# A YOCO decoder step on one core: the last three output tiles by halves of the tokens

## The chip, the cores and the metric

The kernel runs on one core of one Trainium2 chip. The metric is the device time of one execution in microseconds (us), as a median of several runs; beside it stands one execution that was recorded by the hardware profiler, and all rows of the profile come from that one. Its "span" is the time from the first to the last instruction of the core.

## What is computed

One inference step of a two-layer decoder over 512 prompt tokens and 8 sample tokens (520 columns in all), width 1024, hidden width 2816. Each layer adds half a SwiGLU, a mixer, and half a SwiGLU again; the kernel works through four SwiGLU blocks, and the fourth is followed by the last RMSNorm, whose rows are the outputs `y_prompt` and `y_sample`:

```python
def _rmsnorm(x, g):
    xf = x.astype(jnp.float32)
    y = xf * lax.rsqrt(jnp.mean(xf * xf, axis=-1, keepdims=True) + EPS)
    return (y * g.astype(jnp.float32)).astype(x.dtype)
...
        x = x + 0.5 * _swiglu(_rmsnorm(x, norm_g[l, 2]), ffn_w_gate[l, 1], ffn_w_up[l, 1], ffn_w_down[l, 1])
    y = _rmsnorm(x, final_norm_g)
```

Everything is float32. The sum of squares over the width of 1024 can be known only when all of a token's outputs are there.

## The kernel before

The activations lie transposed: `x[m]` (m = 0 to 7) holds 128 of the 1024 features in the partitions and the 520 tokens in the columns, and `H` = 260 is half of the tokens. A product in full precision is three matmuls, since activations and weights are each split into a high and a low part (`th`/`tl`, `hh`/`hl`, `wh`/`wl`); `mm` (L406) issues the three terms for one slice of weights, each for the two halves of the tokens, into the two banks of a pair. There are four such pairs of PSUM banks, handed out by `duo` (L224); a pair is free again when all that reads it is done. Transposes and sums for 1/rms take pairs from the same four.

**Weights.** `Weights` (L95) loads chunks of weights into three buffers `raw` and splits them, piece by piece, into six buffers `wh` and six `wl` (ScalarE at L191, VectorE at L192). `get` hands out the next piece, `prefetch` splits up to five pieces ahead. A piece's buffer is free for the sixth next one when its matmuls are done.

**One SwiGLU block** is `ffn` (L556). It goes through the hidden width in three parts of 8, 8 and 6 tiles; in each part it computes the hidden tiles (`plain_tile`, `strassen_tile`, with the matmuls at L435), then adds the part's share to all eight output tiles (the matmuls at L410). The first two output tiles are interleaved, so that the last hidden tile is needed late (L573 to L584); the others go one by one through `mm_tile` (L418). For each tile, L589 scales the result by 1/rms of the block's input (`u`, from PSUM) and L590 adds it to `x[m]`. In the last part, `after(m)` is called for each tile. With six hidden tiles an output tile of the last part takes 6 x 3 x 2 = 36 matmuls of 260 columns and two pieces of weights.

**The end of the kernel.** In the fourth block `after` is `final_after` (L1265). For tile k it takes the squares on ScalarE (`square`, L363), adds them to `acc` on VectorE (L367), and scales `x[k]` by the norm's weight into `xg` (ScalarE, L1268). Then it calls `turn` (L1245) for the tile that waits, and lets tile k wait. So tile 0 is turned when tile 1 is through, and so on. `turn` transposes one `xg` on TensorE, four times 128 tokens (L1250) and a last 120 (L1251), and copies the five results from PSUM to the output rows `yt`, by turns on VectorE (L1261) and ScalarE (L1259). After the last turn, `rstd_tok` (L372) sums the squares over the partitions with five small matmuls (L378) and computes 1/rms of all tokens in twelve tiny VectorE operations (L382 to L389). At last, ten half rows are scaled in place (VectorE L1283, ScalarE L1281) and stored, one DMA each, half of them from SyncE's queue and half from ScalarE's (L1287, L1289).

**What sets the order.** The kernel is written in an order of its own, but each engine's queue is filled by the framework's scheduler, which simulates the program and may put an instruction ahead of others that it takes to be ready later. `later` (L248) pins an instruction behind all that was written before it for its engine. Once the queues are fixed, each engine works through its own in order; an instruction whose data aren't there holds up all behind it.

## Time and profile before

| what | value |
|---|---|
| time, median of 3 runs | 1728.08 us (1722.71 to 1731.19) |
| the profiled execution, its own time | 1729.8 us |
| its span | 1728.0 us |
| mean granted clock of TensorE | 0.98 |
| TensorE busy (PE) | 97% of the span |
| VectorE (DVE), ScalarE (ACT) busy | 73%, 52% |
| DMA | 227.06 MB, mean 131 GB/s |

How to read the rows below: in the timeline, a row is start, duration, engine, line, operation, output and inputs, and in brackets how long the engine stood idle before it and what ended that. In the chain, a row is start, time on the path in us, engine, output and line (with the count of instructions merged into it). In the stretches, there follow on each stretch its length, the busy time of PE, PEld (weight loads), DVE, ACT and POOL with their instructions, the granted clock of TensorE, the DMA engines' busy share and GB/s. In the groups, a row is line, engine, operation, tiles, shapes and count, then busy us and the mean of one in ns, then the idle time before. ACTq and SPq are the queues from which ScalarE and SyncE issue DMAs.

### The profile page before, as it was taken

How to read it: one execution, taken by the hardware profiler on the slowest of the kernel's cores; microseconds unless marked ns; L12 is line 12 of the kernel's file. 1: busy time of each engine (PE TensorE's matmuls, PEld its weight loads, DVE VectorE, ACT ScalarE, POOL GpSimd, SP SyncE). 2: the span in 40 equal slices, each digit the busy share in tenths (PEclk: the TensorE clock that was granted, in tenths of full speed). 3: DMA queues.
4: the chain of work that ended last, by engine and by line, in shares of the span. 5: the costliest groups of instructions: out<-in, count | busy, mean ns of one | idle time of the engine just before them, and what ended most of it. 6: DMA issues, size and time to landing. Idle time of an engine off the chain costs nothing.

```text
span 1728.0 us, 34367 instructions
## 1 busy us (share of the span) xinstructions
PE 1669.6 (97%) x13701; PEld 1654.0 (96%) x13701; DVE 1269.1 (73%) x2454; ACT 904.7 (52%) x1810; POOL 146.1 (8%) x178
## 2 busy tenths in 40 slices
PE   7999999999899999999999999998889999999996
PEld 7999999999899999999999999998779899999996
DVE  6966866877875875887866866878756785785765
ACT  6643634656552643655543634647855653462553
POOL 0101101001001101001101101100000110110100
PEclk9999999999999999999999999999979999999998
DMA  8646746663445845546646746642112465666531
GB/s 204 159 129 141 171 135 144 180 183 75 102 141 132 182 134 135 141 128 145 155 127 141 174 135 141 155 140 50 25 35 73 111 163 144 146 150 159 135 86 51
DMA packets 315872, 227.06 MB, mean 131 GB/s; under 512 B 9265, under 2 KB 290969, under 8 KB 315671
## 3 DMA queue, kind: packets, MB, share of 16 engines
q1 hardware_dynamic: 285872, 174.82, 35.5%
q0 software_dynamic: 23200, 41.82, 14.7%
q10 hardware_dynamic: 6638, 8.23, 1.5%
q8 instruction: 107, 1.75, 0.4%
q14 instruction: 55, 0.44, 0.1%
HBM read 180.89 MB, written 5.04 MB: 108 GB/s over the span
## 4 chain that ended last, share of the span: by engine, by line
PE 67%; DVE 4%; ACT 3%; issue 0%; ACTq 0%; DVEq 0%
PE ps L435 35%; PE ps L410 30%; ACT sm L1034 1%; DVE sm L1019 1%; PE ps L1075 1%; DVE wl L192 1%; PE ps L1159 0%; PE ps L1052 0%; DVE xl L243 0%; ACT xh L242 0%; PE ps L1127 0%; DVE rp L856 0%; ACT wh L191 0%; PE ps L1250 0%; ACT oT L1087 0%
## 5 line engine op out<-in xcount | busy, mean ns | idle before, releaser
L191 ACT ACTIVATE wh<-raw 128x512 fp32r<-128x512 f32 (+1 forms) x742 | 449.6, 621 | 542.8 <-PE ps L410 326.3
L192 DVE TENSOR_TENSOR wl<-raw,wh 128x512 fp32r<-128x512 f32 (+1 forms) x742 | 491.0, 677 | 206.9 <-ACT wh L191 202.2
L435 PE MATMUL ps<-th,wh 128*128 128x260 f32 x1264 | 358.4, 284 | 5.4 <-ACT th L242 3.7
L435 PE MATMUL ps<-tl,wh 128*128 128x260 f32 x1264 | 358.7, 284 | 0.4 <-DVE tl L243 0.4
L435 PE MATMUL ps<-th,wl 128*128 128x260 f32 x1264 | 356.5, 283 | 0.6 <-DVE wl L192 0.5
L410 PE MATMUL ps<-hh,wh 128*128 128x260 f32 x1376 | 282.1, 286 | 4.0 <-DVE mx L1019 3.0
L410 PE MATMUL ps<-hl,wh 128*128 128x260 f32 x1376 | 280.9, 284 | 0.0
L410 PE MATMUL ps<-hh,wl 128*128 128x260 f32 x1376 | 279.4, 283 | 0.0
L435 PEld LDWEIGHTS ps<-th,wh 128*128 128x128 f32 x1264 | 238.9, 189 | 6.7 <-ACT th L242 4.1
L435 PEld LDWEIGHTS ps<-tl,wh 128*128 128x128 f32 x1264 | 239.4, 189 | 1.3 <-DVE tl L243 1.3
L435 PEld LDWEIGHTS ps<-th,wl 128*128 128x128 f32 x1264 | 238.6, 189 | 1.0 <-DVE wl L192 1.0
L410 PEld LDWEIGHTS ps<-hh,wh 128*128 128x128 f32 x1376 | 213.4, 190 | 5.4 <-DVE mx L1019 3.6
L410 PEld LDWEIGHTS ps<-hl,wh 128*128 128x128 f32 x1376 | 215.0, 190 | 0.0
L410 PEld LDWEIGHTS ps<-hh,wl 128*128 128x128 f32 x1376 | 214.0, 189 | 0.0
L435 PE MATMUL ps<-xh,wh 128*128 128x260 f32 x708 | 198.9, 283 | 0.6 <-ACT wh L191 0.6
L435 PE MATMUL ps<-xl,wh 128*128 128x260 f32 x708 | 198.6, 283 | 0.0
L435 PE MATMUL ps<-xh,wl 128*128 128x260 f32 x708 | 194.7, 282 | 1.0 <-DVE wl L192 1.0
L156 POOL DMA_DIRECT2D raw<-raw x79 | 68.4, 866 | 1389.1 <-DVE wl L192 504.7
L589 DVE TENSOR_TENSOR u<-ps,R 128x520 f32<-128x520 f32 x96 | 67.0, 698 | 107.5 <-PE ps L410 107.5
L435 PEld LDWEIGHTS ps<-xh,wh 128*128 128x128 f32 x708 | 133.6, 189 | 1.0 <-ACT wh L191 0.8
L435 PEld LDWEIGHTS ps<-xl,wh 128*128 128x128 f32 x708 | 133.5, 189 | 0.0
L435 PEld LDWEIGHTS ps<-xh,wl 128*128 128x128 f32 x708 | 131.4, 189 | 1.4 <-DVE wl L192 1.4
(237 smaller groups left out, 2845.7 us busy)
## 6 DMA issues: line engine op xcount, KB each, us to landing
raw<-in_ffn_w_gate_dram SPq DMA_DIRECT2D x87, 512.0 KB, 4.1
raw<-in_ffn_w_up_dram SPq DMA_DIRECT2D x87, 512.0 KB, 5.4
raw<-in_ffn_w_down_dram SPq DMA_DIRECT2D x32, 1024.0 KB, 4.9
raw<-raw POOLq DMA_DIRECT2D x79, 256.0 KB, 3.3
S<-in_ffn_w_up_dram SPq DMA_DIRECT2D x79, 256.0 KB, 5.5
S<-raw POOLq DMA_DIRECT2D x79, 256.0 KB, 4.6
raw<-in_ffn_w_down_dram SPq DMA_DIRECT2D x16, 768.0 KB, 6.2
raw<-in_w_q_dram SPq DMA_DIRECT2D x8, 512.0 KB, 6.7
```

The source lines that it names most:

```text
L156: G.dma_start(blk(raw, 2, 1), blk(raw, 1, 1), accum_op=ALU.add)
L191: nc.scalar.activation(dh, src, AF.Copy)
L192: nc.vector.tensor_tensor(dl, src, dh.bitcast(F32), op=ALU.subtract)
L410: T.matmul(banks[:, hf, :H], a[:, kk, :], hcols(b, hf), start=(first and i == 0), stop=(last and i == 2),)
L435: T.matmul(bank[:, :H], a[:, kk, :], b, start=(not more and kk == 0 and i == 0), stop=(kk == 3 and i == 2), skip_group_check=more,)
L589: V.tensor_tensor(halves(u), banks[m][:, :, :H], halves(R), op=ALU.mult)
L1019: V.tensor_tensor_reduce(out=sm[:, e * 256 : (e + 1) * 256], in0=self.pe[e][:, bi * 256 : (bi + 1) * 256], in1=cst[:, mk : mk + 256], op0= ...
L1034: S.activation(part(i), part(i), AF.Exp, bias=nm[:, i : i + 1], accum_out=den[:, i : i + 1])
L1075: T.matmul(po[:, bi * 256 : (bi + 1) * 256], a, p_[:, kc_], start=(n == 0), stop=(n == 3 * len(kts) - 1),)
```

## The change

`ffn` takes a further argument, `by_halves`. In the last part of the fourth block the tiles 0 to 4 go as before. Tiles 5 to 7 (`NH` = 3) are computed for the first 260 columns, each with its own addition to `x` and its call of `by_halves(m, 0)`, and then for the other 260 with `by_halves(m, 1)`; their six pieces of weights and three bank pairs are kept from the first pass to the second. The pairs of all tiles from 2 on are now taken one at a time rather than two at a time.

Two tiles wait before one is turned (three in the list before the first is taken), so tile 0 is turned when tile 2 is through. `turn` can do a range of token blocks; its copies from one bank are a single operation, on VectorE for even tiles and ScalarE for odd ones, and the block of 120 is copied by the other engine. `final_half` does squares, sum and `xg` of one half; in the first halves it turns the tiles 3 and 4, and the first two token blocks of 5 and 6; behind tile 5's second half follow those of tile 7 and 1/rms of those 256 tokens (`rstd_tok(0, 2)`); behind tile 6's second half those rows are scaled and stored, and the remaining blocks of tiles 5, 6 and 7 are turned one behind the other. At the end `rstd_tok(2)` and the stores of blocks 4, 2 and 3 follow.

```diff
@@ -369,24 +370,22 @@
     pss_ = [None]
     nsb = [4]
 
-    def rstd_tok():
+    def rstd_tok(t0=0, t1=5):
 
         pss_[0] = duo()
         pss = pss_[0][:, 0, :]
-        for t in range(5):
+        for t in range(t0, t1):
             lo = t * P if t < 4 else 400
             T.matmul(pss[:, t : t + 1], acc[:, lo : lo + P], ones[:, 0:1], start=True, stop=True)
-        v = cp.tile([P, 5], F32, tag="nv", name="nv")
-        y = cp.tile([P, 5], F32, tag="ny", name="ny")
-        t1 = cp.tile([P, 5], F32, tag="nt", name="nt")
-        later(V.tensor_scalar(v, pss[:, :5], 1.0 / D, EPS, op0=ALU.mult, op1=ALU.add))
+        v, y, t_ = (cp.tile([P, 5], F32, tag=n, name=n)[:, t0:t1] for n in ("nv", "ny", "nt"))
+        later(V.tensor_scalar(v, pss[:, t0:t1], 1.0 / D, EPS, op0=ALU.mult, op1=ALU.add))
         V.tensor_scalar(y.bitcast(I32), v.bitcast(I32), 1, None, op0=ALU.arith_shift_right)
         V.tensor_scalar(y.bitcast(I32), y.bitcast(I32), -1.0, float(0x5F3759DF), op0=ALU.mult, op1=ALU.add)
         for it in range(3):
-            V.tensor_tensor(t1, y, y, op=ALU.mult)
-            V.scalar_tensor_tensor(t1, t1, -0.5, v, op0=ALU.mult, op1=ALU.mult)
-            o = r_tok[:, :5] if it == 2 else y
-            V.scalar_tensor_tensor(o, t1, 1.5, y, op0=ALU.add, op1=ALU.mult)
+            V.tensor_tensor(t_, y, y, op=ALU.mult)
+            V.scalar_tensor_tensor(t_, t_, -0.5, v, op0=ALU.mult, op1=ALU.mult)
+            o = r_tok[:, t0:t1] if it == 2 else y
+            V.scalar_tensor_tensor(o, t_, 1.5, y, op0=ALU.add, op1=ALU.mult)
 
     def rstd_all():
 
@@ -553,7 +552,7 @@
             split(tt[k + 4], t34)
             yield
 
-    def ffn(fi, tmp, mov, hooks, tt, tags, after, before_last=None):
+    def ffn(fi, tmp, mov, hooks, tt, tags, after, before_last=None, by_halves=None):
 
         j = 0
         for pi, n in enumerate(PARTS):
@@ -568,30 +567,47 @@
                     strassen_tile(tmp, mov, tt, hs)
                 j += 1
             nk = (n + 1) // 2
-            for m0 in range(0, KT, 2):
-                banks = {m: duo() for m in (m0, m0 + 1)}
-                if m0 == 0:
-                    late = []
-                    for m in (0, 1):
-                        for k0, k1 in ((0, nk), (nk, n)):
-                            w = W.get()
-                            for k in range(k0, min(k1, n - 1)):
-                                mm(w, k - k0, hs[k], banks[m], k == 0, False)
-                            finish()
-                        late.append((w, m))
-                    for w, m in late:
-                        mm(w, n - 1 - nk, hs[n - 1], banks[m], False, True)
-                    W.prefetch()
-                for m in (m0, m0 + 1):
-                    if m0:
-                        mm_tile(hs, banks[m])
-                    u = tmp.tile([P, TOK], F32, tag="sb", name="u", bufs=nsb[0])
-                    V.tensor_tensor(halves(u), banks[m][:, :, :H], halves(R), op=ALU.mult)
-                    V.scalar_tensor_tensor(x[m], u, -0.5, x[m], op0=ALU.mult, op1=ALU.add)
-                    if last:
-                        if before_last is not None:
-                            next(before_last, None)
-                        after(m)
+            rest = NH if last and by_halves is not None else 0
+
+            def add(m, bank, hfs):
+                c = slice(hfs[0] * H, (hfs[-1] + 1) * H)
+                u = tmp.tile([P, TOK], F32, tag="sb", name="u", bufs=nsb[0])[:, c]
+                parts = lambda z: z.rearrange("p (h c) -> p h c", c=H)
+                V.tensor_tensor(parts(u), bank[:, hfs[0] : hfs[-1] + 1, :H], parts(R[:, c]), op=ALU.mult)
+                V.scalar_tensor_tensor(x[m][:, c], u, -0.5, x[m][:, c], op0=ALU.mult, op1=ALU.add)
+
+            banks = {m: duo() for m in (0, 1)}
+            late = []
+            for m in (0, 1):
+                for k0, k1 in ((0, nk), (nk, n)):
+                    w = W.get()
+                    for k in range(k0, min(k1, n - 1)):
+                        mm(w, k - k0, hs[k], banks[m], k == 0, False)
+                    finish()
+                late.append((w, m))
+            for w, m in late:
+                mm(w, n - 1 - nk, hs[n - 1], banks[m], False, True)
+            W.prefetch()
+            for m in range(KT - rest):
+                if m > 1:
+                    banks[m] = duo()
+                    mm_tile(hs, banks[m])
+                add(m, banks[m], (0, 1))
+                if last:
+                    if before_last is not None:
+                        next(before_last, None)
+                    after(m)
+
+            ws = {}
+            for hf in range(2 if rest else 0):
+                for m in range(KT - rest, KT):
+                    if not hf:
+                        banks[m] = duo()
+                        ws[m] = W.get(), W.get()
+                    for k in range(n):
+                        mm(ws[m][k // nk], k % nk, hs[k], banks[m], k == 0, k == n - 1, (hf,))
+                    add(m, banks[m], (hf,))
+                    by_halves(m, hf)
 
     def ff_pool():
         return tc.tile_pool(name="ff", bufs=2)
@@ -1240,53 +1256,82 @@
     kvs.close()
 
     with ff_pool() as tmp:
-        tt, yt = {}, {}
-
-        def turn(k, xg):
+        tt = {}
+
+        yt = [tmp.tile([P, 4, 512], F32, name="yt", bufs=1)]
+        ys = []
+        xgs, waiting = {}, []
+
+        def turn(k, t0=0, t1=5):
 
             pd = duo()
             pa, pb = pd[:, 0, :], pd[:, 1, :]
-            for t in range(4):
-                T.transpose(pa[:, t * P : (t + 1) * P], xg[:, t * P : (t + 1) * P], ident)
-            T.transpose(pb[:120, :P], xg[:, 400:520], ident)
-            for t in range(5):
-                n = P if t < 4 else 120
-                if k % 4 == 0:
-                    yt[t, k // 4] = big.tile([P, 512], F32, tag=XX[k // 4], name="yt")
-                dst = yt[t, k // 4][:n, (k % 4) * P : (k % 4 + 1) * P]
-                src = pa[:, t * P : (t + 1) * P] if t < 4 else pb[:120, :P]
-                if t % 2:
-                    S.copy(dst, src)
-                else:
-                    V.tensor_copy(dst, src)
-
-        waiting = []
+            for t in range(t0, min(t1, 4)):
+                T.transpose(pa[:, t * P : (t + 1) * P], xgs[k][:, t * P : (t + 1) * P], ident)
+            if t1 > 4:
+                T.transpose(pb[:120, :P], xgs[k][:, 400:520], ident)
+            if k == 4 and len(yt) < 2:
+                yt.append(rawp.tile([P, 4, 512], F32, tag="raw", name="yt1"))
+            if t1 > 4 and k % 4 == 0:
+                ys.append(big.tile([P, 512], F32, tag=XX[k // 4], name="ys"))
+            cols = slice((k % 4) * P, (k % 4 + 1) * P)
+            dst = yt[k // 4][:, t0 : min(t1, 4), cols]
+            src = pa.rearrange("p (t c) -> p t c", t=4)[:, t0 : min(t1, 4), :]
+            one, other = (S.copy, V.tensor_copy) if k % 2 else (V.tensor_copy, S.copy)
+            one(dst, src)
+            if t1 > 4:
+                other(ys[k // 4][:120, cols], pb[:120, :P])
+
+        def scaled(k, c):
+            if k not in xgs:
+                xgs[k] = tmp.tile([P, TOK], F32, tag=("t", "sa")[k % 2], name="xg")
+            S.activation(xgs[k][:, c], x[k][:, c], AF.Copy, scale=gcol(N_FIN, k))
 
         def final_after(k):
             square(k, tmp, "g")
-            xg = tmp.tile([P, TOK], F32, tag="t", name="xg")
-            S.activation(xg, x[k], AF.Copy, scale=gcol(N_FIN, k))
-            if waiting:
-                turn(*waiting.pop())
-            waiting.append((k, xg))
-
-        ffn(3, tmp, mov6, start_hooks(tmp, 5, tt, 1), tt, HH, final_after)
-        turn(*waiting.pop())
-        rstd_tok()
-        for t in range(5):
-            n = P if t < 4 else 120
-            for a in range(2):
-                y = yt[t, a][:n, :]
-                if a:
-                    S.activation(y, y, AF.Copy, scale=r_tok[:n, t : t + 1])
-                else:
-                    V.tensor_scalar(y, y, r_tok[:n, t : t + 1], None, op0=ALU.mult)
-                cols = slice(a * 512, (a + 1) * 512)
-                eng = nc.sync if a else nc.scalar
-                if t < 4:
-                    eng.dma_start(y_prompt[0, t * P : (t + 1) * P, cols], y)
-                else:
-                    eng.dma_start(y_sample[:, 0, cols], yt[t, a][112:120, :])
+            scaled(k, slice(0, TOK))
+            waiting.append(k)
+            if len(waiting) > 2:
+                turn(waiting.pop(0))
+
+        def store(tiles):
+            for t in tiles:
+                n = P if t < 4 else 120
+                for a in range(2):
+                    y = yt[a][:, t, :] if t < 4 else ys[a][:120, :]
+                    if a:
+                        S.activation(y, y, AF.Copy, scale=r_tok[:n, t : t + 1])
+                    else:
+                        V.tensor_scalar(y, y, r_tok[:n, t : t + 1], None, op0=ALU.mult)
+                    cols = slice(a * 512, (a + 1) * 512)
+                    eng = nc.sync if a else nc.scalar
+                    if t < 4:
+                        eng.dma_start(y_prompt[0, t * P : (t + 1) * P, cols], y)
+                    else:
+                        eng.dma_start(y_sample[:, 0, cols], ys[a][112:120, :])
+
+        def final_half(k, hf):
+            c = slice(hf * H, (hf + 1) * H)
+            sq = tmp.tile([P, TOK], F32, tag="g", name="sq")
+            S.activation(sq[:, c], x[k][:, c], AF.Square)
+            V.tensor_tensor(acc[:, c], acc[:, c], sq[:, c], op=ALU.add)
+            scaled(k, c)
+            if not hf and waiting:
+                turn(waiting.pop(0))
+            if (k, hf) > (KT - NH, 0) and not hf:
+                turn(k - 1, 0, 2)
+            if (k, hf) == (KT - NH, 1):
+                turn(KT - 1, 0, 2)
+                rstd_tok(0, 2)
+            elif hf:
+                if k == KT - NH + 1:
+                    store((0, 1))
+                turn(k - 1, 2)
+
+        ffn(3, tmp, mov6, start_hooks(tmp, 5, tt, 1), tt, HH, final_after, by_halves=final_half)
+        turn(KT - 1, 2)
+        rstd_tok(2)
+        store((4, 2, 3))
 
 
 # ---- launch: one core; inputs and outputs as the reference has them ----
```

More of the change, by code (lines that the diff above doesn't have):

```diff
@@ L29 @@
 LAG = 2
+NH = 3
 NPL = (3, 2, 2, 2)
```

## The prediction

> **What bounds the kernel now.** I read the page first, for the engine that is never idle; then the timeline of TensorE and the stretches of the last 55 us, the only part that the change touches; then the chain that ended last, from the last matmul to the end.
>
> ```profile
> PE 1669.6 (97%) x13701; PEld 1654.0 (96%) x13701; DVE 1269.1 (73%) x2454; ACT 904.7 (52%) x1810; POOL 146.1 (8%) x178
> ```
>
> TensorE is the bound nearly everywhere, so work that leaves another engine is worth nothing by itself. What can be won is TensorE's own waiting, and the stretch after its last matmul. In the timeline of TensorE, where tile 1 of the last pass ends and tile 2 should begin:
>
> ```profile
> 1675.49 0.40 PE L410 MATMUL ps<-hh,wl 128*128 128x260 f32 x2
> 1679.18 1.11 PE L1250 MATMUL ps<-ident,xg 128*128 128x128 f32 x4 [3.29 <-ACT xg L1268]
> ...
> 1680.16 0.78 PE L410 MATMUL ps<-hh,wh 128*128 128x260 f32 x2
> ...
> 1684.64 0.60 PE L410 MATMUL ps<-hl,wh 128*128 128x260 f32 x2
> 1685.07 0.41 PE L410 MATMUL ps<-hh,wl 128*128 128x260 f32 x2
> ```
>
> TensorE stands still for 3.29 us: the transposes of tile 0 are queued ahead of tile 2's products and wait for xg. Afterwards pairs of matmuls take 0.64 instead of 0.40 us until about 1684.9. The chain of waits gives the price, with tile 3 below it as the undisturbed case, and the stretches give the granted clock (third figure from the right):
>
> ```profile
> 1679.18 1.11 PE ps L1250 x4
> 1680.29 0.21 PE ps L1251
> 1680.51 6.39 PE ps L410 x36
> 1686.90 0.44 PE ps L1250 x4
> 1687.34 0.11 PE ps L1251
> 1687.45 4.29 PE ps L410 x36
> ```
> ```profile
> 1676.00:1687.00 11.00, 7.82 (x44) 7.82 (x45) 5.45 (x13) 4.03 (x9) 0.00 (x0) 0.69 0.01 2
> 1687.00:1692.00 5.00, 5.00 (x45) 5.00 (x43) 3.89 (x9) 2.79 (x7) 0.00 (x0) 1.00 0.00 0
> ```
>
> A turn and a tile cost 0.44 + 0.11 + 4.29 = 4.84 us at clock 1.00, but 1.11 + 0.21 + 6.39 = 7.71 us here. So this place holds 3.29 + 2.87 = 6.16 us. Then the end, in the chain after the last matmul:
>
> ```profile
> 1706.82 4.31 PE ps L410 x36
> ...
> 1711.15 0.70 DVE u L589
> ...
> 1712.05 0.62 DVE x L590
> ...
> 1712.75 0.64 ACT sq L363
> 1713.39 0.63 ACT xg L1268
> ...
> 1714.06 0.66 PE ps L1250 x4
> ...
> 1718.52 0.18 DVE r_tok L389
> ```
>
> The last matmul ends at 1706.82 + 4.31 = 1711.13, and from there everything is serial: 2.93 us to the first transpose, then transposes with copies that alternate between DVE and ACT, then 1/rms until 1718.70. That is 7.57 us; the stores take the 9.30 us from there to the span's end at 1728.0.
>
> **The change, part by part.**
>
> *A, the turns lag by one tile more.* The queue of waiting tiles now holds two before one is popped, so tile 0's transposes stand behind tile 2's products. Those need a free pair of banks (tiles 0 and 1 hold two of four) and pieces 4 and 5 of the weights. Counted back from the last split, the split of piece 5 is this, with its low half on DVE right after, long before the stall:
>
> ```profile
> 1667.85 0.53 ACT L191 ACTIVATE wh<-raw 128x384 fp32r<-128x384 f32 x1 [0.48 <-PE ps L410]
> 1668.41 0.56 DVE L192 TENSOR_TENSOR wl<-raw,wh 128x384 fp32r<-128x384 f32 x1 [0.57 <-ACT wh L191]
> ```
>
> So tile 2 starts at 1675.89 and ends at 1680.2, and xg of tile 0, on which the turn waited until 1679.18, is early for that. A = 6.16 us, and nothing that the profile shows is late next.
>
> [...]
>
> *B, tiles 5 to 7 by halves on TensorE.* Each product already covers 260 columns and loads its own weights, so the count stays 36 per tile. Half-wide sequences run no slower in the chain:
>
> ```profile
> 1669.67 1.45 PE ps L435 x12
> ```
>
> That is 0.121 us each against 4.29/36 = 0.119. What moves ahead of the last matmul is the first two of five transposes of tiles 6 and 7 (2 x 2/5 x 0.55 = 0.44 us) and two of the five sums for 1/rms (4 of 10 matmuls, below: 0.47 us). B = -0.91 us.
>
> ```profile
> 1714.66 1.17 PE L378 MATMUL ps<-ones,acc 128*128 128x1 f32 x10
> ```
>
> *C, the serial stretch up to 1/rms.* Its operations shrink from 520 to 260 columns. Rows of that width or near it:
>
> ```profile
> L528 DVE TENSOR_TENSOR g<-ps,t 128x260 f32<-128x260 f32 x79 | 33.8, 428 | 20.9 <-PE ps L435 19.1
> L516 ACT COPY sa<-ps 128x260 f32<-128x260 f32 x79 | 28.3, 358 | 0.0
> L797 ACT ACTIVATE hx<-x,gT 128x120 f32<-128x120 f32 x8 | 2.4, 381 | 0.9 <-DVE acc L367 0.9
> L1268 ACT ACTIVATE xg<-x,gT 128x520 f32<-128x520 f32 x8 | 5.7, 714 | 0.0
> ```
>
> u and x take 0.43 each; the square lies between the plain copy, 0.36, and half a microsecond, and I take 0.42; xg by the line between 381 ns at 120 and 714 at 520 columns takes 0.50, of which 0.08 lie beside the square as in the old chain. With that chain's gaps (0.02, 0.02, 0.08, 0.05) the sum is 0.02 + 0.43 + 0.02 + 0.43 + 0.08 + 0.42 + 0.42 + 0.05 = 1.87 us from the last matmul to the first transpose, not 2.93. In the old order five transposes and ten small matmuls take from 1714.06 to 1715.83, 1.77 us; three and six take some 1.2. The copies, which went on until nv started at 1716.32, become one ACT copy of 256 columns (under 0.4 us, as L516) beside one on DVE, both hidden by the small matmuls. The twelve tiny DVE steps stay, 2.38 us:
>
> ```profile
> 1716.32 0.15 DVE L382 TENSOR_SCALAR nv<-ps 128x5 f32<-128x5 f32 x1
> ```
>
> 1.87 + 1.2 + 0.04 + 2.38 = 5.5 against 7.57: C = 2.1 us.
>
> *D, the stores.* The stretches around the stores (last two figures: DMA share, GB/s) and the traffic of the last 9 us:
>
> ```profile
> 1719.50:1720.00 0.50, 0.00 (x0) 0.00 (x0) 0.50 (x3) 0.50 (x2) 0.00 (x0) 0.50 0.00 0
> 1720.50:1721.00 0.50, 0.00 (x0) 0.00 (x0) 0.29 (x1) 0.50 (x2) 0.00 (x0) 0.50 1.04 385
> 1725.50:1726.00 0.50, 0.00 (x0) 0.00 (x0) 0.00 (x0) 0.00 (x0) 0.00 (x0) 0.50 0.46 86
> ```
> ```profile
> q1 hardware_dynamic: 592, 1.07, 32.7%
> q10 hardware_dynamic: 592, 1.07, 32.4%
> ```
>
> The engines are full (share over 1) from 1720 to 1725.6: 2.14 MB at some 385 GB/s, 5.5 us. Eight stores of 256 KB and two of 16 KB make it up; four of the eight, 1.05 MB or 2.7 us, leave the end. The tail's order is now tile 4 first, whose stores are small, so large ones begin one DVE scaling (about 0.4 us) later. D = 2.7 - 0.4 = 2.3 us. The moved stores issue on SP, which holds no other load by then, and on ACT's queue, between squares and scalings. An issue there is on the old chain with this:
>
> ```profile
> 1719.24 0.35 ACTq L1287
> ```
>
> Two of them cost ACT, half idle in this stage, between nothing and 0.7 us; I take nothing.
>
> *E, what the half stage costs DVE and ACT, and who waits.* Halving costs 2 x 0.43 - 0.70 = 0.16 us per DVE operation, nine times, 1.4 us; the second 1/rms chain costs 2.4 us; fewer, wider copies give back some 2.9 us (three copies of 0.29 in each of eight turns become about 4.1 us by the same line of 0.43 at 260 and 0.70 at 520 columns). DVE does that inside some 16 us, in stretches that were this busy (third figure):
>
> ```profile
> 1692.00:1697.00 5.00, 5.00 (x45) 5.00 (x44) 3.88 (x9) 2.69 (x7) 0.00 (x0) 1.00 0.00 0
> 1702.00:1707.00 5.00, 5.00 (x44) 5.00 (x44) 2.85 (x8) 1.68 (x4) 0.00 (x0) 1.00 0.00 0
> ```
>
> I count 13 to 14 us of DVE work there, over 80%. Three new waits follow. First, nv (L382) is pinned behind the squares' sum of tile 5's second half, and the chain behind it delays u and x of tile 6; TensorE needs those only for a turn two products later. Second, the turns of a first half need an xg whose product ended only one product (2.15 us) and a few transposes before, against the 1.87 us worked out above plus any queue on DVE; behind the turn stand the next half's products. Third, tiles 5, 6 and 7 hold three of the four bank pairs from first to second half, so the next turn or the sums must wait until the copies of the last one are out. Nothing here shows these waits. The lower bound is zero; DVE idles before each u today. The upper bound is five turns that each hold the only pair as long as tile 6's did in the old order:
>
> ```profile
> 1710.95 0.60 PE L1250 MATMUL ps<-ident,xg 128*128 128x128 f32 x4
> ...
> 1714.19 0.29 DVE L1261 COPY yt<-ps 120x128 f32<-120x128 f32 x1
> ```
>
> That is 3.53 us each, 17.6 in all. Below zero is excluded: no part of E takes work off TensorE. I take 1.3 us, near the lower end: three waits of about 0.3 us, and 0.4 us of DVE queue at the last matmul.
>
> **Sum.** 6.16 - 0.91 + 2.1 + 2.3 - 1.3 = 8.35 us. The profiled execution took 1729.8 us with a span of 1728.0; it would become 1721.4 with 1719.6. The median shown, 1728.08, lies 1.7 below that execution; from it the forecast is 1719.7 us.
>
> **Rivals.**
>
> *R1, the turn still stands in TensorE's way.* The framework's scheduler sets each queue's order; if it puts tile 0's turn, or a half's, in front of products that are ready, another stall of 3.3 us at a falling clock returns. For it: in the old order it put a turn whose data were 3.29 us off ahead of tile 2. Against it: that turn stood first in the program as well. Price: A is lost, gain 2.2, 1725.9 us.
>
> *R2, the first half's 1/rms comes too late,* so the change doesn't do what it says. The second halves' products wait for nothing but weights, so the scheduler may run them early, and the first half's sums, chain and stores then fall into the tail. D goes, and the chain of 2.4 us comes before its twin: gain 8.35 - 2.3 - 2.4 = 3.7, 1724.4 us. Against it: the sums come ahead of two products in the program.
>
> *R3, slower: the bank pairs.* If each of the five takes of the last pair waits for a whole hold of 3.53 us, TensorE stalls 17.6 us instead of 1.3, and the time is 1728.08 - 8.35 + 16.3 = 1736.0. It decides for slower than before from waits of about 9.7 us in all, some 2 us per take. Against it: the combined copies last 0.4 to 0.7 us, where the old hold came of five that took turns.
>
> **How the numbers follow.** Forecast 0.68, R1 0.13, R2 0.13, R3 0.06. A measurement of this kernel can tell about 0.5%, 8.6 us, from no change, and the forecast of 8.35 lies just short of it. With E at zero the gain is 9.65, with E at 3 it is 6.65; of the forecast's 0.68 I give 0.42 to gains over 8.6. R1 and R2 lie within 0.5%. R3 decides for slower by over 0.5% with 0.05, 0.01 of it stays within. So faster 0.42, same 0.53, slower 0.05. The range: the runs of before spread from 1722.71 to 1731.19, so medians may move some 3 us; 1714 is the forecast with E at zero and that movement, 1727 takes in R1 and R2 and leaves R3 out.
>
> **What would show it.** A: no idle TensorE near 1676, clock 1.00 there, tile 2 directly after tile 1. B: the last product ends near 1711.1 - 6.2 + 0.9 + 0.9 = 1706.8. C: r_tok some 5.5 to 5.9 us later. D: two blocks of store traffic, half of it ahead of the last product, and about 7 us from r_tok to the end. E: TensorE rows at L1250, L378 or L410 with idle time before them between 1690 and 1707. It is wrong if an idle of over 1 us stands there, or if the rows before 1660 moved, since nothing else of the program was meant to change.

## The result and the profile after

The kernel with the change takes 1720.62 us (median of 8 runs, 1718.18 to 1722.40) against 1728.63 us for the kernel before (median of 8 runs beside it): a ratio of 0.9953, 95% interval 0.9938 to 0.9968. That is 8.0 us, 0.47%. The interval lies clear of 1; the gain is just under the 0.5% that the prediction took as what a measurement of this kernel can tell from no change. The forecast was 1719.7 us.

The profiled execution took 1720.47 us with a span of 1718.7. Its rows start 0.84 us ahead already before the changed part. The prediction named moved rows before 1660 as a sign of being wrong; they aren't one, since two profiles of the unchanged kernel (e9 and e10) lie 7.64 us apart at this place. So spans aren't compared directly below: I count from the start of the last hidden tile's matmuls (the last row `L434 x12`, in the kernel before `L435 x12`), the anchor. Up to there TensorE, VectorE and ScalarE work through the same operations in the same order in both kernels. From there to the end the kernel before took 1728.0 - 1669.67 = 58.33 us, the changed one 1718.7 - 1668.83 = 49.87: 8.46 us less, where the forecast had 8.35.

The chain of waits after the change (start, us, what), the same places as before:

```profile
1668.83 1.45 PE ps L434 x12
1670.28 9.08 PE ps L409 x76
1679.36 0.44 PE ps L1270 x4
1679.79 0.11 PE ps L1272
1679.90 4.30 PE ps L409 x36
...
1696.89 4.80 PE ps L409 x40
1701.72 1.10 DVE u L576 x3
...
1707.13 0.44 PE ps L1270 x2
1707.57 0.12 PE ps L1272
```

Tiles 0 to 2 now run without a gap, and the turn and tile that took 7.71 us take 4.85. The stretches say the same (third figure from the right: granted clock; the last two: DMA share and GB/s):

```profile
1676.00:1687.00 11.00, 11.00 (x96) 11.00 (x95) 9.88 (x20) 7.47 (x15) 0.00 (x0) 1.00 0.01 2
1697.00:1702.00 5.00, 4.90 (x42) 4.66 (x40) 0.30 (x2) 0.30 (x1) 0.00 (x0) 1.00 0.00 0
1710.50:1711.00 0.50, 0.00 (x0) 0.00 (x0) 0.43 (x3) 0.00 (x0) 0.00 (x0) 0.50 0.99 369
...
1713.00:1713.50 0.50, 0.00 (x0) 0.00 (x0) 0.36 (x1) 0.50 (x2) 0.00 (x0) 0.50 0.63 201
...
1716.00:1716.50 0.50, 0.00 (x0) 0.00 (x0) 0.00 (x0) 0.00 (x0) 0.00 (x0) 0.50 1.01 385
```

First row: clock 1.00 and TensorE busy all 11 us (7.82 and 0.69 before). Second row: TensorE is busy for 4.90 of 5 us while VectorE does 0.30 us of work; that is odd, and it is the key to the rest. Last rows: the stores do leave in two blocks with a dip near 1713, but both lie behind the last product. VectorE's timeline shows why:

```profile
1701.72 1.10 DVE L576 TENSOR_TENSOR u<-ps,R 128x260 f32<-128x260 f32 x3 [4.70 <-PE ps L409]
...
1704.67 0.43 DVE L576 TENSOR_TENSOR u<-ps,R 128x260 f32<-128x260 f32 x1 [0.16 <-PE ps L409]
...
1705.69 0.15 DVE L381 TENSOR_SCALAR nv<-ps 128x2 f32<-128x2 f32 x1
...
1708.91 0.16 DVE L388 SCALAR_TENSOR_TENSOR r_tok<-nt,ny 128x2 f32<-128x2 f32 x1
1708.98 0.15 DVE L381 TENSOR_SCALAR nv<-ps 128x3 f32<-128x3 f32 x1
1709.10 0.88 DVE L1305 TENSOR_SCALAR yt<-yt,r_tok 128x512 f32<-128x512 f32 x2
1709.90 0.16 DVE L382 TENSOR_SCALAR ny<-nv 128x3 int32<-128x3 int32 x1
...
1711.88 0.16 DVE L388 SCALAR_TENSOR_TENSOR r_tok<-nt,ny 128x3 f32<-128x3 f32 x1
```

The scheduler didn't keep the written order. On TensorE it put all of tile 5's and tile 6's second halves ahead of tile 7's first half; on VectorE the `u` of tile 7's first half stands ahead of those of the second halves. So VectorE waits for 4.70 us, then has three `u` at once, and the first half's 1/rms (nv with 2 columns) starts only at 1705.69, when the last product (its last row starts at 1704.35 and takes 0.28 us) is already over. Its twelve steps, the two scalings and the second chain (3 columns) share one queue in the tail.

### The profile page after: what moved, and what is told of

It reads as the page before. It is cut to its first block, busy times and chain, and to the rows that moved or that the text cites. A ratio compares the mean times of both kernels' runs of the same rounds, so it can differ in the third digit from the quotient of the medians.

```text
span 1718.7 us, 34382 instructions
## 1 busy us (share of the span) xinstructions
PE 1667.1 (97%) x13701; PEld 1651.3 (96%) x13701; DVE 1267.9 (74%) x2460; ACT 905.5 (53%) x1810; POOL 146.0 (8%) x178
## 4 chain that ended last, share of the span: by engine, by line
PE 67%; DVE 4%; ACT 2%; issue 0%; ACTq 0%; DVEq 0%
PE ps L434 35%; PE ps L409 30%; DVE sm L1035 1%; ACT sm L1050 1%; PE ps L1091 1%; DVE wl L193 1%; DVE xl L244 0%; PE ps L1068 0%; PE ps L1175 0%; PE ps L1143 0%; ACT xh L243 0%; DVE rp L872 0%; ACT wh L192 0%; ACT oT L1103 0%; DVE tl L244 0%
## 5 line engine op out<-in xcount | busy, mean ns | idle before, releaser
L434 PE MATMUL ps<-th,wh 128*128 128x260 f32 x1264 | 358.2, 284 | 5.4 <-ACT th L243 3.7
L434 PE MATMUL ps<-tl,wh 128*128 128x260 f32 x1264 | 358.7, 284 | 0.5 <-DVE tl L244 0.5
L434 PE MATMUL ps<-th,wl 128*128 128x260 f32 x1264 | 356.5, 283 | 0.6 <-DVE wl L193 0.5
L434 PEld LDWEIGHTS ps<-th,wh 128*128 128x128 f32 x1264 | 238.8, 189 | 6.7 <-ACT th L243 4.1
L434 PEld LDWEIGHTS ps<-tl,wh 128*128 128x128 f32 x1264 | 239.3, 189 | 1.3 <-DVE tl L244 1.3
L434 PEld LDWEIGHTS ps<-th,wl 128*128 128x128 f32 x1264 | 238.6, 189 | 1.0 <-DVE wl L193 1.0
L434 PE MATMUL ps<-xh,wh 128*128 128x260 f32 x708 | 199.0, 283 | 0.6 <-ACT wh L192 0.6
L434 PE MATMUL ps<-xl,wh 128*128 128x260 f32 x708 | 198.7, 283 | 0.0
L434 PE MATMUL ps<-xh,wl 128*128 128x260 f32 x708 | 194.7, 282 | 1.0 <-DVE wl L193 1.0
L576 DVE TENSOR_TENSOR u<-ps,R 128x520 f32<-128x520 f32 (+1 forms) x99 | 67.1, 681 | 108.8 <-PE ps L409 108.8
L434 PEld LDWEIGHTS ps<-xh,wh 128*128 128x128 f32 x708 | 133.7, 189 | 1.0 <-ACT wh L192 1.0
L434 PEld LDWEIGHTS ps<-xl,wh 128*128 128x128 f32 x708 | 133.7, 189 | 0.0
L434 PEld LDWEIGHTS ps<-xh,wl 128*128 128x128 f32 x708 | 131.5, 189 | 1.4 <-DVE wl L193 1.4
```

The lines of the kernel that those rows point to most:

```text
L434: T.matmul(bank[:, :H], a[:, kk, :], b, start=(not more and kk == 0 and i == 0), stop=(kk == 3 and i == 2), skip_group_check=more,)
L576: V.tensor_tensor(parts(u), bank[:, hfs[0] : hfs[-1] + 1, :H], parts(R[:, c]), op=ALU.mult)
```

## The experiments

All runs in one table. "Last product" is counted from the anchor above, "r_tok" from the end of the last product to the end of the last step of 1/rms, "end" from there to the end of the span; the three add up to "total". Ratios are to the kernel before, with their 95% intervals, from 6 to 12 timed executions of each; e9, e10 and e11 are single executions, taken for their profiles.

| kernel | last product | r_tok | end | total | ratio |
|---|---|---|---|---|---|
| before | 41.45 | 7.57 | 9.31 | 58.33 | |
| before, second profile (e9) | 40.14 | 8.61 | 9.20 | 57.95 | |
| before, third profile (e10) | 40.24 | 8.47 | 9.20 | 57.91 | |
| the change | 35.80 | 7.41 | 6.66 | 49.87 | 0.9953 (0.9938 to 0.9968) |
| e1, the lag alone | 34.75 | 7.63 | 9.22 | 51.60 | 0.9972 (0.9956 to 0.9988) |
| e2, written order pinned | 37.57 | 6.13 | 6.67 | 50.37 | 0.9956 (0.9940 to 0.9973) |
| e3, one 1/rms at the end | 35.80 | 6.82 | 9.65 | 52.27 | 0.9966 (0.9950 to 0.9982) |
| e4, before with the gap filled | 38.55 | 7.57 | 9.25 | 55.37 | 0.9998 (0.9983 to 1.0014) |
| e5, the halves without the lag | 39.58 | 7.24 | 6.70 | 53.52 | 0.9990 (0.9975 to 1.0004) |
| e11, e5 profiled again | 39.58 | 7.25 | 6.67 | 53.50 | |
| e6, first scalings on ScalarE | 35.80 | 6.71 | 7.30 | 49.81 | 0.9951 (0.9934 to 0.9969) |
| e7, pinned, first scalings on ScalarE | 37.57 | 7.41 | 6.32 | 51.30 | 0.9963 (0.9947 to 0.9979) |
| e8, a shorter first chain | 35.80 | 6.40 | 6.62 | 48.82 | 0.9942 (0.9926 to 0.9958) |
| e12, first scalings on GpSimd | 35.80 | 7.50 | 7.40 | 50.70 | 0.9967 (0.9954 to 0.9981) |

The ratios tell all but e4 and e5 from the kernel before, but hardly from each other; what tells the mechanisms apart is the three columns of the traces, which repeat to a few hundredths where the clock is full.

**My theory** was that the lag gives most of the gain, by ending TensorE's stall and the slow clock behind it, and that the halves give the rest in the tail, less than forecast because the first half's 1/rms and scaling lie in VectorE's queue there. **The rivals**: the halves alone remove the stall; the late tail comes of the scheduler's order of products; or the clock has nothing to do with the stall.

### The lag alone, and the halves without it

```diff
-            xg = tmp.tile([P, TOK], F32, tag="t", name="xg")
+            xg = tmp.tile([P, TOK], F32, tag=("t", "sa")[k % 2], name="xg")
...
-            if waiting:
-                turn(*waiting.pop())
             waiting.append((k, xg))
+            if len(waiting) > 2:
+                turn(*waiting.pop(0))
```

> The kernel before with the lag of two tiles alone, no halves and the old copies. Theory (the idle TensorE at tile 1 and the falling clock behind it are part A, 6.16 us): the idle of 3.29 us and the 0.64 us pairs vanish, the last product ends some 6 us earlier; three turns instead of two now stand behind the last product, so the tail may be up to 0.7 us longer: 5.5 to 6.2 us faster than before, ratio 0.9964 to 0.9968. Rival (most of the gain comes from the halves and the early stores): 0 to 2 us faster, ratio above 0.9988.

The chain of the kernel before with the lag alone:

```profile
1666.95 9.08 PE ps L410 x76
1676.03 0.44 PE ps L1250 x4
...
1695.95 4.32 PE ps L410 x36
```

No gap, and full speed behind it (granted clock 1.00 from 1676 to 1700). From the anchor to the end it is 6.3 to 6.7 us shorter than the kernel before; the timed ratio, 0.9972, is 4.8 us, with an interval of 2.1 to 7.6. One turn more (0.55 us) now lies behind the last product, so the lag gave 41.45 - 34.75 - 0.55 = 6.15 us against the execution from which the forecast was made. Of the change's 8.46 us, the halves are the last 51.60 - 49.87 = 1.73, together with the wider copies of `turn`, which e1 doesn't have and which no run separates from the halves.

The other way round, in the changed kernel:

```diff
-            if len(waiting) > 2:
+            if len(waiting) > 1:
```

> The changed kernel with the old lag (one tile waits, not two), halves kept. My theory: tile 0's turn stands ahead of tile 2's products again, TensorE idles some 3.3 us near the start of tile 2 and its clock falls below 0.8 for the stretch after it; from the start of the last hidden product to the end 49.87 + 6.2 = about 56 us, time 0.998 to 0.999 of the kernel before. Rival (the halves, with banks taken one pair at a time, remove the wait by themselves and the lag is nothing): no idle over 0.5 us there, clock 1.00, about 50 us, 0.995.

The same wait of tile 0's turn is back in the timeline of TensorE, but the stretch behind it, this time, is at full clock:

```profile
1677.49 0.66 PE L1270 MATMUL ps<-ident,xg 128*128 128x128 f32 x4 [3.29 <-ACT xg L1288]
```
```profile
1676.00:1687.00 11.00, 9.51 (x80) 9.51 (x81) 6.67 (x13) 5.98 (x11) 0.00 (x0) 1.00 0.01 2
```

So the rival falls (the halves don't remove the stall), and my number falls too: 53.52 us, 3.65 more than with the lag, where 6.2 more was expected. (The timed ratio, 0.9990, lies where I expected it, but its interval leaves room for both.) The idle time came back and the slow clock didn't.

### The clock behind the gap

In the kernel before, 27 matmuls of 260 columns whose result nothing reads, put into the gap, pinned ahead of tile 0's transposes:

```diff
+            if k == 0:
+                for i in range(27):
+                    later(T.matmul(pb[:, 128 : 128 + H], tt[1][0][:, :P], hcols(tt[0][0], 0), start=True, stop=True))
```

> The kernel before with 27 matmuls of 260 columns that nothing reads (extra work, the result unused) ahead of tile 0's transposes, where TensorE stood idle 3.29 us. They take about 3.2 us. Theory (the slow stretch behind the idle time, 2.87 us, comes from the clock falling when TensorE stands still): the pairs of tile 2 take 0.40 us and the granted clock from 1676 to 1687 is 1.00; 2.9 us faster than before in spite of the extra work, ratio 0.9983. Rival (the slow stretch has another cause, the transposes or the order): the 0.64 us rows stay, ratio 1.000.

```profile
1677.76 3.24 PE ps L1251 x27
1681.00 2.77 PE ps L410 x23
1683.77 0.44 PE ps L1253 x4
```

With the gap filled, 23 matmuls take 2.77 us, 0.120 each: full speed. The last product comes 41.45 - 38.55 = 2.90 us earlier, as expected, though TensorE did nothing useful in the gap. The scheduler also put these 23 matmuls of tile 2 ahead of the transposes, so the order changed as well; but in e5 the transposes follow the gap as in the kernel before, at full clock, so neither they nor their place make the slow stretch. With TensorE busy throughout there is none: the granted clock is 1.00 from 1676 to 1700. The timed ratio, 0.9998 (0.9983 to 1.0014), can neither show nor exclude 2.9 us.

Then the kernel before twice again, and the halves without the lag once more, one profiled execution each.

> The kernel before, unchanged, profiled a second time. In its first profile TensorE stood still for 3.29 us ahead of tile 0's turn and then ran at half clock for 5.7 us; with the lag undone in the changed kernel the same 3.29 us were followed by full clock. Theory (whether the clock falls after a gap of this length differs from execution to execution): the gap is 3.2 to 3.4 us again, and the stretch after it is either at 1.00 (start of the last hidden product to the end 55.4 us) or at half clock (58.3 us), not in between. Rival (the clock always falls in this kernel): 58.3 us each time.

> The kernel before, unchanged, profiled a third time, for the same question: 55.4 us (full clock after the gap of 3.29 us) or 58.3 us (half clock) from the start of the last hidden product to the end by the theory of chance, always 58.3 by the rival.

> The changed kernel with the lag undone, profiled a second time, for the same question: 53.5 us (full clock after the gap) or about 56.4 us (half clock) from the start of the last hidden product to the end by the theory of chance; by the rival (the clock does not fall in the halves version) always 53.5.

The second profile of the kernel before, in three views: the gap in the timeline, the tile behind it in the chain, and the clock by stretches:

```profile
1674.36 0.90 PE L1250 MATMUL ps<-ident,xg 128*128 128x128 f32 x3 [3.29 <-ACT xg L1268]
```
```profile
1675.69 5.07 PE ps L410 x36
...
1709.26 1.94 PE ps L378 x10
```
```profile
1670.42:1673.83 3.41, 0.65 (x6) 0.44 (x4) 3.19 (x6) 1.80 (x4) 0.00 (x0) 1.00 0.00 0
1673.83:1677.24 3.41, 2.88 (x14) 2.88 (x15) 2.16 (x6) 2.16 (x5) 0.00 (x0) 0.50 0.00 0
...
1709.00:1711.00 2.00, 2.00 (x12) 2.00 (x10) 0.88 (x3) 0.53 (x2) 0.00 (x0) 0.50 0.00 0
```

The gap is 3.29 us every time, to the hundredth. But the rows behind it were slow for 5.7 us in the first profile and until 1677.24, 2.88 us, here: tile 0's turn and tile 2 together take 1680.76 - 1674.36 = 6.40 us, 1.56 over the undisturbed 4.84 (third profile 6.51, 1.67 over). And the clock fell once more behind the last product, in the wait for the last xg, so that the ten small matmuls took 1.94 us and 1/rms came 1.0 us later (0.9 in the third, with a mean clock of 0.56 from 1715.5 to 1718.5). My theory of "55.4 or 58.3, nothing in between" is wrong, as is the rival's 58.3 each time: the totals are 57.95 and 57.91. The halves without the lag gave 53.50, full clock again (1.00 from 1676 to 1687).

So the clock loss behind a gap of 3.29 us was 2.87, 1.56, 1.67, 0 and 0 us. With the gap filled (e4) or gone (e1) there was none. What goes with its size can be read from the traces' records of the clock. In those of the kernel before (the first profile) and of the change, the clock changes only in steps of 3.41 us: every stretch of one clock between two changes is a whole multiple of that (in the first profile half clock from 1678.24 to 1685.07, two steps, then full clock for 30.72 us, nine; in the changed kernel full clock for 327.68 us up to 1708.34, 96). The half clock behind the gap of e9, 1673.83 to 1677.24, lasts one such step. Here are the steps at the gap in the first profile, and in e5, where they are counted back from the change at 1713.62:

```profile
1674.83:1678.24 3.41, 1.06 (x9) 0.85 (x8) 2.79 (x6) 1.42 (x3) 0.00 (x0) 1.00 0.00 0
1678.24:1681.65 3.41, 2.47 (x12) 2.47 (x13) 2.30 (x6) 2.46 (x6) 0.00 (x0) 0.50 0.00 0
1681.65:1685.07 3.42, 3.42 (x17) 3.42 (x17) 0.80 (x2) 0.63 (x2) 0.00 (x0) 0.50 0.00 0
```
```profile
1672.66:1676.07 3.41, 1.54 (x14) 1.33 (x12) 2.30 (x5) 1.05 (x2) 0.00 (x0) 1.00 0.00 0
1676.07:1679.49 3.42, 2.00 (x17) 2.00 (x18) 2.80 (x6) 2.56 (x5) 0.00 (x0) 1.00 0.00 0
```

In all five profiles the gap reaches over the edge of a step. A step's length less TensorE's busy time (the first figure behind the length) gives the share of the gap that lies in it:

| profile | idle in the first step | idle in the second | steps at half clock | loss, us |
|---|---|---|---|---|
| before | 2.35 | 0.94 | 2 | 2.87 |
| e9 | 2.76 | 0.53 | 1 | 1.56 |
| e10 | 3.03 | 0.26 | 1 | 1.67 |
| e5 | 1.87 | 1.42 | 0 | 0 |
| e11 | 1.84 | 1.45 | 0 | 0 |

Where most of the first step was idle, the clock fell at its end, and it stayed low for one step more where the second had 0.94 us of idle time; where the edge cut the gap nearer its middle, the clock stayed. That fits all five profiles, but no run moved the gap on purpose, so it is a reading and not a test. Idle time isn't the whole measure: in e1's tail the clock fell behind a step with 1.85 us of it, whose other 1.56 us were transposes and matmuls of one column (mean clock 0.68 from 1700 to 1712).

### The tail: what delays the second half's 1/rms

The written order, enforced by a pin on the first matmul of each half product:

```diff
-                T.matmul(
+                ins = T.matmul(
...
+                if pin and i == 0:
+                    later(ins)
```

> The changed kernel, with the first matmul of each half product pinned behind what was written before it for TensorE, so that the halves run in the order of the program and not, as the scheduler had it, with the second halves pulled ahead. Theory (the tail did not shrink because VectorE idled 4.7 us while the products of the first halves came late, and did the first 1/rms in the tail): VectorE's idle of 4.7 us is gone, the first r_tok is there before the last product ends, the stretch from the last product to the second r_tok falls from 7.4 to some 5.7 us; TensorE does 0.7 us more ahead of its last product and waits some 0.5 us: 0.5 us faster than the changed kernel, ratio to before near 0.9950. Rival (the tail is long for a reason of its own, the order does not matter): the stretch stays above 7 us and the kernel is 1 us slower than the changed one, ratio near 0.9960.

VectorE's timeline in the pinned kernel; the last product ends at 1704.50:

```profile
1700.44 0.15 DVE L381 TENSOR_SCALAR nv<-ps 128x2 f32<-128x2 f32 x1
...
1704.03 0.16 DVE L388 SCALAR_TENSOR_TENSOR r_tok<-nt,ny 128x2 f32<-128x2 f32 x1
1704.23 0.88 DVE L1307 TENSOR_SCALAR yt<-yt,r_tok 128x512 f32<-128x512 f32 x2
1705.03 0.42 DVE L578 TENSOR_TENSOR u<-ps,R 128x260 f32<-128x260 f32 x1
...
1710.46 0.17 DVE L388 SCALAR_TENSOR_TENSOR r_tok<-nt,ny 128x3 f32<-128x3 f32 x1
```

This is what the prediction described: the first 1/rms is there 0.31 us before the last product ends, and the second 6.13 us after it, of which 0.53 is the last `u`, queued behind the first half's two scalings. Without these, 5.60, the 5.5 that the prediction worked out. The price lies on TensorE: the last product ends 37.57 - 35.80 = 1.77 us later, since parts of two turns and the sums go ahead of it and it waits 0.76 us in all, not 0.30. So the order does set the tail, as the theory says, but the total, 50.37, is 0.50 us longer than with the scheduler's order, where the theory had 0.5 us shorter.

One 1/rms for all tokens and all stores at the end, products as in the changed kernel:

```diff
-                rstd_tok(0, 2)
...
-                if k == KT - NH + 1:
-                    store((0, 1))
...
-        rstd_tok(2)
-        store((4, 2, 3))
+        rstd_tok()
+        store((4, 0, 1, 2, 3))
```

> The changed kernel without the early part: one sum and one 1/rms of all tokens and all stores at the end, halves and lag as they are. Theory (as the queues stand, the first 1/rms and its stores fall into the tail, so they win little): all stores behind r_tok cost some 2.6 us more, the first chain of 1/rms out of the tail saves some 1.7 us: about 1 us slower than the changed kernel, ratio to before near 0.996. Rival (the early 1/rms and stores give what they say): 3 us or more slower than the changed kernel, ratio 0.997 or more.

It is 2.40 us longer than the change, nearer the rival's 3 than the theory's 1: 1/rms ends 0.59 us earlier (VectorE has only one chain to do), but the stores take 9.65 us, 2.99 more. Even behind the last product the early stores are worth more than their chain costs. Without them the halves are worth less than nothing: 52.27 against 51.60 for the lag alone.

Then VectorE's load was taken away piece by piece. The four scalings of the first half all on ScalarE, behind the last turn:

```diff
-                    if a:
+                    if a or t < 2:
                         S.activation(y, y, AF.Copy, scale=r_tok[:n, t : t + 1])
...
         turn(KT - 1, 2)
+        store((0, 1))
         rstd_tok(2)
```

> The changed kernel with all four scalings of the first half on ScalarE and behind the last turn, none on VectorE. Theory (VectorE's queue is what makes the second r_tok late: the two scalings of 0.44 us lie inside the second chain of twelve steps, and the first chain ahead of it makes nv 0.65 us late): the second chain takes 2.4 instead of 3.07 us, last product to second r_tok 6.7 to 6.8 us instead of 7.42; ScalarE's four scalings end near the same time, so the gain at the end is 0.3 to 0.7 us. Rival (the second chain is slowed by something else, or the turns on TensorE set it): last product to r_tok stays at 7.3 to 7.5 us and the end does not come earlier, or comes later because ScalarE has two scalings more.

1/rms ends 6.71 us after the last product, 0.70 earlier, as expected. But the end hardly moved (49.81, where 0.3 to 0.7 us were expected): ScalarE has two scalings of about 0.6 us more to do before it reaches those of the second half, and "end" grows by 0.64.

The first chain with one Newton round instead of three:

```diff
-        for it in range(3):
+        for it in range(2 if t1 == 2 else 0, 3):
```

> The changed kernel with one Newton round instead of three in the first half's 1/rms only (six VectorE steps of about 0.2 us fewer; those 256 tokens are scaled with a coarser 1/rms). Theory (the first chain lies in the tail on VectorE and pushes the second): nv of the second chain starts 0.2 to 0.5 us earlier and the scalings go ahead of it rather than inside it, last product to second r_tok 6.4 to 6.7 us instead of 7.42, end about 0.8 us earlier (49.0 to 49.3). Rival (the first chain lies beside other work, as forecast, and costs nothing): 7.3 to 7.5 us and 49.9.

```profile
1707.94 0.15 DVE L381 TENSOR_SCALAR nv<-ps 128x3 f32<-128x3 f32 x1
...
1710.12 0.16 DVE L388 SCALAR_TENSOR_TENSOR r_tok<-nt,ny 128x3 f32<-128x3 f32 x1
```

The second chain starts 4.06 us after the last product (4.35 in the changed kernel) and is done 6.40 after it, and the total falls by 1.05 us to 48.82. The two scalings now stand ahead of the second chain and not inside it. Six tiny steps of 0.2 us were worth nearly their 1.2 us: the first chain lay on the path that sets the end. It is the fastest kernel here, but with less arithmetic, and its interval overlaps that of the change.

The pinned order with the scalings on ScalarE (the diffs of e2 and e6 together):

> The kernel with the second halves' products pinned in the written order, and the first half's scalings all on ScalarE behind the last turn. Theory (VectorE's queue): u of the last half product comes 0.9 us earlier after the last product than in the pinned kernel (3.0 us late there, 2.1 to 2.2 here, since the rest of the first chain is still ahead of it), last product to second r_tok about 7.7 us instead of 8.6, from the start of the last hidden product to the end 49.4 to 49.7 instead of 50.37. Rival (the wait is for TensorE or ScalarE): u is as late as before, 8.5 us or more, 50.3 or more.

The 3.0 us in that expectation were misread: they were counted from the product before the last one, and `u` in the pinned kernel is 0.53 us late. It is now 0.04 us behind the last product, so VectorE's scalings were what it waited for. But the chain shows what is late next:

```profile
1709.62 0.48 ACT yt L1305
1710.10 0.14 issue
1710.23 1.08 ACT yt L1305 x2
1711.32 0.14 issue
1711.45 0.40 ACT sq L1318
```

The scheduler put all four scalings (1708.99 to 1711.55, the first two of them in part under the row that the chain calls issue) ahead of the last square on ScalarE, and 1/rms came 7.41 us after the last product instead of 6.13. The total, 51.30, is 0.93 us longer than in e2, where the theory had it shorter.

The two scalings of VectorE on GpSimd, idle there:

```diff
-                        V.tensor_scalar(y, y, r_tok[:n, t : t + 1], None, op0=ALU.mult)
+                        (nc.gpsimd if t < 2 else V).tensor_scalar(y, y, r_tok[:n, t : t + 1], None, op0=ALU.mult)
```

> The changed kernel with the two scalings of the first half that VectorE does moved to GpSimd, idle there; ScalarE keeps its two. By what the runs so far showed (the scalings lie inside the second chain on VectorE) the second r_tok ends 6.7 us after the last product instead of 7.41, as with all four on ScalarE, and since ScalarE is not loaded the end follows 6.6 to 6.7 us later, not 7.3: 49.2 us from the start of the last hidden product to the end instead of 49.87. Rival (GpSimd takes several us for 128x512 and its two stores, issued behind it from ScalarE's queue, are late): the end 7.3 us or more after r_tok, 49.9 or more.

The timelines of GpSimd and of VectorE:

```profile
1705.65 3.11 POOL L1305 TENSOR_SCALAR yt<-yt,r_tok 128x512 f32<-128x512 f32 x2 [68.42 <-DVE nv L381]
```
```profile
1705.74 0.61 DVE L383 TENSOR_SCALAR ny<-ny 128x3 int32<-128x3 int32 x1
1706.39 0.16 DVE L385 TENSOR_TENSOR nt<-ny 128x3 f32<-128x3 f32 x1
...
1707.44 0.47 DVE L388 SCALAR_TENSOR_TENSOR ny<-nt,ny 128x3 f32<-128x3 f32 x1
```

Both parts of the expectation fail. GpSimd takes 1.56 us per scaling where VectorE takes 0.44, so the stores are late (end 7.40). And while GpSimd runs, two of VectorE's tiny steps take 0.61 and 0.47 us instead of 0.17: 1/rms isn't earlier at all (7.50 us). It is 0.8 us slower than the change.

## Why the prediction was right, and where it was wrong

**A, the lag (6.16 us): right, with a size that varies.** e1 measures 6.15 against the execution from which the term was taken. Against the other two profiles it gives 40.14 - 34.75 - 0.55 = 4.84 and 4.94 us, since the half clock lasted one step there and not two. The 3.29 us of idle time are firm; the 2.87 us of slow clock were one draw. That the total of the kernel before hardly differs, 57.9 to 58.3, is because in those two the clock fell again behind the last product. Against their mean, 57.93, the change gains 8.06 us, and by the medians 8.0. Of these 8.06, about 1 us is that second fall, which the prediction didn't have: that the sum held for these executions too was luck.

**B and the waits of E (last product at 41.45 - 6.16 + 0.91 + 0.9 = 37.1 us): 35.80.** In the written order it is 37.57, so the working was near, but the kernel doesn't run in that order. The scheduler put second-half products ahead, one wait of 0.30 us on TensorE is all that is left, and the rest of tile 5's turn, the first blocks of tile 7's and the sums went behind the last product.

**C with the queue of E (1/rms 5.5 + 0.4 us after the last product): 7.41. This is the step that failed.** The prediction took the first half's 1/rms and scaling for work beside the second half's products. That was rival R2's case, given 0.13, and its mechanism is what happened: second halves ran early and the first chain fell into the tail. The 1.5 us can be read off: the first transpose of the last half comes at 2.50 us, not 1.87 + 0.4; nv of the second chain, which should come 1.2 us later, comes 1.85 later, behind the first chain; and the second chain takes 3.06 us, not 2.38, with the first half's two scalings inside it. e6 gave back 0.70 by taking the scalings out, e8 1.01 by shortening the first chain; e2 shows 6.13 in the written order.

R2's price, 4.7 us, wasn't paid. The chains overlap with transposes and copies instead of standing one behind the other, and the first stores still leave 3 us ahead of the second's, so that D stayed.

**D, the stores (2.3 us): 2.65,** 9.31 to 6.66 us from 1/rms to the end, although no store left ahead of the last product.

So that the sum, 8.35, came so close to 8.46 was in part luck, since two misses offset each other: the last product 1.3 us earlier than forecast, 1/rms 1.5 us later, the stores 0.35 shorter. R1 and R3 didn't occur: no stall near 1676, and one wait of 0.30 us on TensorE, for a `u`, not 17.6 us for bank pairs. One sum of the prediction doesn't come out: E at zero and a movement of 3 us give 1728.08 - 9.65 - 3 = 1715.4 as the lower end of the range, not 1714; nothing hangs on it.

## What to carry to other kernels

Before a gain "beside" other work is counted, ask whether the scheduler has any reason to keep the written order; here the second halves of two tiles were moved ahead, and what was to be hidden beside them landed in the tail. Count a tail by its queues: six steps of 0.2 us, taken out ahead of the last chain on the same engine, gave back 1.05 us (e8), and two scalings of 0.44, taken out of that chain, brought 1/rms 0.70 us earlier (e6). Moving them to another engine won nothing at the end here: ScalarE had the second half's scalings behind them ("end" grew by 0.64), and GpSimd took 1.56 us for each (e12). And a stall of TensorE is priced from several executions, since the slow clock behind the same gap of 3.29 us cost from 0 to 2.87 us in five profiles; in these it went with where the gap lay in the steps of the clock.

## What the runs showed of the hardware

The start of the last hidden tile moved between 1664.85 and 1672.49 us in executions of the same unchanged kernel (e9 and e10), nearly as much as the whole gain. Most of it, 6.0 of the 7.64 us, arises far ahead of the change, between 1246 and 1300 us: the same instructions of VectorE lie 1.08 us apart in the two profiles ahead of it and 7.10 behind it. That is in the stretch with the lowest clock, where the second profile was granted 0.90 and the third 0.81:

```profile
1200.00:1300.00 100.00, 87.50 (x672) 80.23 (x671) 68.60 (x250) 72.47 (x222) 0.00 (x0) 0.90 0.13 33
```
```profile
1200.00:1300.00 100.00, 88.33 (x617) 81.16 (x618) 65.30 (x243) 68.37 (x214) 0.00 (x0) 0.81 0.14 33
```

So the times of these two executions, 1724.57 and 1732.13 us, differ by 7.56 us while their tails differ by 0.04. Counting from an anchor behind that stretch is what made differences of half a microsecond readable.

GpSimd's scalings stretched single tiny steps of VectorE from 0.17 to 0.61, 0.47 and 0.22 us (e12), while the other steps beside them kept 0.16 to 0.17. All three lie within the first 0.7 us of one of the two scalings, which start at 1705.65 and 1707.21. That the two engines get in each other's way is what the rows suggest; by what, no run shows. The longest delay, 0.44 us, is well short of one of GpSimd's scalings, 1.56.
